# The fourth bank of x: normed one stage earlier, turned in 32 by 32 blocks by VectorE and re-laid by DMA instead of by TensorE transposes

## The chip, the cores and the metric

One NeuronCore of one Trainium2 chip runs the whole program in a single launch. The metric is the device time of an execution in microseconds (us). The kernel before takes 2167.93 us as the median of three runs (2167.46 to 2168.04). The profile comes from one more execution, which took 2169.86 us, of which 2168.0 us lie between its first and its last instruction; that is the profile's span.

## The reference

A decoder block for one sequence of 2048 positions and a width of 1024, in float32:

```python
h = rms_norm(x, g_norm) * (1.0 + scale) + shift        # scale, shift from c @ w_mod
proj = h @ w_in                                        # (2048, 1024) @ (1024, 8192)
x_rnn, z_rnn, q, k, v, z_attn, g_r, g_a = split(proj)
# branch A: causal conv, gated linear recurrence over the positions, SiLU gate, w_out_rnn
# branch B: rotary q and k, three dilated windows of attention, SiLU gate, w_out_attn
merged = sigmoid(g_r + bg_r) * y_rnn + sigmoid(g_a + bg_a) * y_attn
x = rms_norm(x + gate * (merged @ w_o), g_final)
```

What matters here is `h`. TensorE contracts over the partitions, so the projections need `h` with its 1024 columns on the partitions and the positions along the free dimension, while `x` lies in memory with the positions as rows. Before the projections, each row of `x` is scaled by its reciprocal root mean square (the norm), the matrix is turned, and each column gets its factor `g` and its shift `s`.

## The kernel before

**Tiles.** The 2048 positions are four banks of 512. A bank is read as four tiles `xs[r]` of 128 positions by 1024 columns, r being the position modulo 4. Column block `k` (0 to 7, 128 columns) of a bank becomes one turned tile of 128 partitions (columns) by 512 positions, in the order r, j. Every operand of a product is kept as a high part (`float32r`, rounded) and a low part (what is left), and each product is three matmuls (line 152): high by high, high by low, low by high.

**Halves and stages.** The work on `w_in` is done twice: `f = 0` for banks 0 and 1, `f = 1` for banks 2 and 3. Each half has these stages:

- *Values* (`values_half`, line 876): the 1024 columns of `v` for both banks, as wide products with `h` as the stationary operand. Weights come by SP's queue into the five tiles R (line 473), and are split by ScalarE (line 160) and GpSimd (line 166) into the seven tiles S. In the same stage the second bank of the half is built (`build_odd`, line 588): its eight column blocks, and from them and the first bank the sums T1 to T4 that the seven products of a Strassen scheme need.
- *Recurrent, gates, plain q and k*: 22 pairs of column tiles, each as seven products of 12 matmuls (`strassen`, line 349).
- *Rotated* (from line 1353): six pairs, 42 products, two of them q and k columns that get the rotary angles. Its order is written out by hand: `late` maps the number of finished products to functions, `later(d, fn)` puts `fn` behind the d-th product from now, and after each product `run_late` (line 220) issues what is due; then come the loads and splits of the next weights (`pump`). So each engine's queue has its instructions in exactly this order, and an instruction that has to wait holds up what stands behind it on its engine. In the second half this stage computes the residual gate; in the first half it prepares bank 2, the first bank of the second half: `next_norm` loads it 3 products in, squares at 7 to 10 (line 1293), scales at 14 to 17 (line 1297), and `next_even` (line 1302) turns and builds it from product 36 on, so that the second half's values can start without a pause.

**The fourth bank before.** Bank 3 is loaded at line 1327 (`load_x`, line 541) when the second half begins. `norm_x` (line 545) norms it during the second half's values: four squares on ScalarE (line 549), the small steps of `rstd` on VectorE, four scalings on VectorE (line 551). Then `turned` (line 555) has TensorE transpose the four 128 by 128 pieces of one column block into PSUM (line 561), 32 transposes for the bank, and `build` (line 564) reads the PSUM tile twice on ScalarE, for the high part (line 571) and for a full copy that is kept (line 574), and has VectorE subtract (line 169). The order of the values stage is not written by hand: a planner orders its instructions by its own estimates of durations, per engine. The first half's odd bank, bank 1, takes the same path.

**After it.** Attention, the output projections and the final norm follow; their order is written by hand too, and counted in products and units, not in time.

The PSUM tiles of the Strassen products are X (two buffers), Z, W, V and Y (one each). V is written by product 4 of a pair, evicted, and then used once more by the pair's last product, which runs as the second product of the next pair; the next V follows two products behind that.

Of the kernel before, what the change touches and what calls it, by code (L numbers as in the profile page):

```python
# [90 lines left out]
def decoder_block(ctx, tc, x, c, positions, g_norm, w_mod, b_mod, w_in, b_gate, conv_w, conv_b,  # L91
# [10 lines left out]
    def scratch(name, shape):  # L102
        return nc.dram_tensor(name, shape, F32, kind="Internal").ap()
# [13 lines left out]
    gateD = scratch("gateD", [1, D])  # L117

    tabD = scratch("tabD", [2, 2, 32, HALF])

    sD = scratch("sD", [REBUILT * 7, P, 2, KH, P])

# [45 lines left out]
    def lo_dve(o, i, h):  # L168
        return nc.vector.tensor_tensor(o, i, h.bitcast(F32), ALU.subtract).ins  # L169
# [375 lines left out]
    def norm_x(st, xs, nb=2):  # L545
        for t in xs:
            jk = T(st, [P, D], BF16, "hf", bufs=nb)
            ss = T(st, [P, 3, 1], F32, "ss", bufs=4)
            nc.scalar.activation(jk[:], t, AF.Square, accum_out=ss[:, 0])
            rstd(ss)  # L550
            nc.vector.tensor_scalar(t, t, ss[:, 1], None, ALU.mult)
# [12 lines left out]
    def build(st, names, xs, k, first=False, keep=None, pt=None):  # L564
# [11 lines left out]
        else:  # L576
            hf = T(st, [P, CH], F32, "hf", bufs=2)
            nc.vector.tensor_scalar(hf[:], pv, g, s, ALU.mult, ALU.add)
            (lo_dve if k % 3 == 0 else lo_pool)(hl[:, k % KH, :], hf[:], hh[:, k % KH, :])

    def operand(name):
        B[name] = (slot(), slot())

# [1 line left out]
        for k in ks:  # L585
            build(st, ("B11", "B21"), xs, k, first)

    def build_odd(st, xs):

        B["B12"] = (T(st, [P, KH, CH], F32R, "b12h"), T(st, [P, KH, CH], F32R, "b12l"))  # L590
        operand("B22")
        f32 = lambda b, i, k: B[b][i][:, k, :].bitcast(F32)
        tt = nc.vector.tensor_tensor
        h = [T(st, [P, CH], F32, "hx", bufs=KT)[:] for _ in range(KT)]
        for k in range(KH):
            for k2 in (k, KH + k):
                build(st, ("B12", "B22"), xs, k2, keep=h[k2])
            yield
        for name in ("T1", "T2", "T3", "T4"):
            operand(name)  # L600

        def split(name, k, t):
            hh, hl = B[name]
            hi_act(hh[:, k, :], t)
            lo_dve(hl[:, k, :], t, hh[:, k, :])

        for k in range(KH):
            h1, h2 = h[k], h[KH + k]
            t = T(st, [P, CH], F32, "t0", bufs=2)[:]
            tt(t, h2, h1, ALU.subtract)  # L610
# [5 lines left out]
            tt(h2, h2, h1, ALU.subtract)  # L616
# [259 lines left out]
    def values_half(f, xs):  # L876

        n0, n1 = banks(f)
        if f:
            first = wide_values(vx, 0, n0, (0, 1))  # L880
            for _ in range(2):
                next(first)
            norm_x(vx, xs)
        else:
            for j in range(KH):
                store_values(vx, 0, n0, j, pv0[j])
            with tc.issue_after(last_copy[0]):
                norm_x(vx, xs)
            first = ()
        odd = build_odd(vx, xs)  # L890
# [12 lines left out]
        assert next(odd, None) is None  # L903
# [343 lines left out]
    def later(d, fn):  # L1247

        late.setdefault(n_prod[0] + d, []).append(fn)
# [32 lines left out]
            later(30 + 2 * q, lambda q=q: total(q))  # L1282
            later(31 + 2 * q, lambda q=q: bias(q))

    def next_norm():

        xs = []
        later(3, lambda: xs.extend(load_x(xp, 2, "x", 2)))
        ss = T(xp, [P, 3, 4], F32, "ss")

        def square(r):
            jk = T(xp, [P, D], BF16, "hf", bufs=2)
            nc.scalar.activation(jk[:], xs[r], AF.Square, accum_out=ss[:, 0, r : r + 1])

        for r in range(4):
            later(7 + r, lambda r=r: square(r))
            later(14 + r, lambda r=r: nc.scalar.activation(xs[r], xs[r], AF.Copy, scale=ss[:, 1, r : r + 1]))
        later(11, lambda: rstd_first(ss))
        later(12, lambda: rstd_last(ss))
        return xs  # L1300

    def next_even():

# [901 lines left out]
```

## Time and profile before

| | |
|---|---|
| runs | 2167.46, 2167.93, 2168.04 us |
| profiled execution | 2169.86 us, span 2168.0 us |
| TensorE (PE) busy | 2138.5 us, 99% of the span |
| VectorE (DVE), ScalarE (ACT), GpSimd (POOL) busy | 1495.3, 1295.4, 1111.4 us |
| rotated stage of the first half | about 571 to 689 us |
| values stage of the second half | about 689 to 781 us |

PE is TensorE's matmuls and PEld its weight loads. SP is the engine that issues most DMAs and does nothing else; SPq names its queue. A row of the timeline has the start, the duration, engine, line, operation, output and input, the number of instructions, and in brackets how long the engine had been idle and what ended that. A matmul's end is modelled, so neighbouring matmuls overlap in the rows: the step from one start to the next is what a matmul costs. A row of the table by stretches has the two ends and the length, then each engine's busy time and the number of its instructions, those that reach over the edges among them.

### The profile page before, as it was taken

What the parts mean: (1) busy time and instruction counts of PE and PEld (TensorE: products, weight loads), DVE (VectorE), ACT (ScalarE), POOL (GpSimd) and SP (SyncE); (2) the same over time, 40 slices, a digit from 0 to 9 for tenths busy, and PEclk for the clock granted to TensorE, in tenths of its full rate; (3) what the DMA queues carried; (4) which work ended last, traced back from release to release, by engine and by line L of the source; (5) the groups of instructions that cost most, each with busy time, mean ns of one, the idle gap of its engine ahead of it and who ended that gap; (6) DMA issues with size and microseconds to landing.
All of it is one profiled execution on the core that took longest, in us unless ns stands there. A gap on an engine that the chain in (4) does not pass through costs nothing.

```text
span 2168.0 us, 32583 instructions
## 1 busy us (share of the span) xinstructions
PE 2138.5 (99%) x10538; PEld 1788.4 (82%) x10539; DVE 1495.3 (69%) x2590; ACT 1295.4 (60%) x2591; POOL 1111.4 (51%) x868
## 2 busy tenths in 40 slices
PE   9999999999999999999999999999999999999998
PEld 6888788888888888888888887888888988878886
DVE  6759877768656725544446584677777787688887
ACT  5748668668644537557547522777877877444333
POOL 1467667677666322223224664466666564422444
PEclk9999999999999999999999999999999999999999
DMA  8467887886655378899996667889886777898553
GB/s 301 144 209 260 278 296 266 284 302 222 175 116 166 113 244 286 294 311 308 326 322 212 161 162 212 279 260 281 263 270 212 244 230 235 298 321 293 181 171 111
DMA packets 416431, 521.39 MB, mean 240 GB/s; under 512 B 107558, under 2 KB 282882, under 8 KB 415236
## 3 DMA queue, kind: packets, MB, share of 16 engines
q1 hardware_dynamic: 376244, 401.65, 59.6%
q10 hardware_dynamic: 34384, 99.78, 12.2%
q0 software_dynamic: 5632, 17.88, 2.5%
q8 instruction: 83, 1.36, 0.2%
q14 instruction: 88, 0.72, 0.1%
HBM read 332.02 MB, written 187.17 MB: 239 GB/s over the span
## 4 chain that ended last, share of the span: by engine, by line
PE 66%; DVE 6%; DMA 5%; ACT 2%; issue 2%; POOL 1%; SPq 0%; POOLq 0%; ACTq 0%; DVEq 0%
PE X L152 13%; PE V L152 13%; PE pj L152 9%; PE Z L152 7%; PE W L152 7%; PE Y L152 6%; PE sc L152 4%; PE o L152 4%; PE pg L152 1%; DMA fg<-mrT 1%; PE pT L1560 1%; DMA fg<-gaT 1%; PE pT L1573 1%; DVE ptl L169 1%; DVE yl L169 1%
## 5 line engine op out<-in xcount | busy, mean ns | idle before, releaser
L166 POOL TENSOR_TENSOR S<-R,S 128x512 fp32r<-128x512 f32 x192 | 295.3, 1545 | 170.1 <-ACT S L160 90.5
L152 PE MATMUL X<-T,S 128*128 128x512 f32 x1344 | 323.9, 390 | 1.5 <-ACT u L385 1.3
L152 PE MATMUL pj<-yh,S 128*128 128x512 f32 x896 | 324.8, 404 | 0.3 <-DVE S L169 0.3
L152 PE MATMUL V<-T,S 128*128 128x512 f32 x1344 | 324.3, 390 | 0.5 <-DVE ev L455 0.5
L152 PEld LDWEIGHTS X<-T,S 128*128 128x128 f32 x1344 | 251.8, 188 | 56.3 <-ACT u L385 2.8
L152 PEld LDWEIGHTS V<-T,S 128*128 128x128 f32 x1344 | 252.0, 188 | 54.4 <-ACT S L160 0.9
L166 POOL TENSOR_TENSOR S<-s,S 128x512 fp32r<-128x512 f32 x116 | 170.4, 1469 | 148.1 <-ACT S L160 112.1
L152 PEld LDWEIGHTS pj<-yh,S 128*128 128x128 f32 x896 | 168.7, 189 | 30.3 <-DVE S L169 1.3
L152 PE MATMUL pj<-yl,S 128*128 128x512 f32 x448 | 176.2, 393 | 0.5 <-POOL yl L166 0.3
L1475 ACT ACTIVATE pp<-pp,st 128x256 f32<-128x256 f32 (+3 forms) x256 | 133.6, 523 | 67.4 <-DVE st L1474 66.1
L160 ACT ACTIVATE S<-s 128x512 fp32r<-128x512 f32 x124 | 77.3, 624 | 143.7 <-DVE s L285 93.2
L152 PE MATMUL W<-T,S 128*128 128x512 f32 x672 | 161.7, 390 | 0.0
L152 PE MATMUL Y<-T,S 128*128 128x512 f32 x672 | 161.6, 390 | 0.0
L152 PE MATMUL Z<-T,S 128*128 128x512 f32 x672 | 161.4, 389 | 0.0
L160 ACT ACTIVATE S<-R 128x512 fp32r<-128x512 f32 x200 | 121.4, 622 | 59.0 <-issue 15.2
L169 DVE TENSOR_TENSOR ptl<-pT,pth 128x384 fp32r<-128x384 f32 (+1 forms) x160 | 97.9, 629 | 76.1 <-ACT pth L160 73.8
L152 PEld LDWEIGHTS W<-T,S 128*128 128x128 f32 x672 | 126.0, 188 | 26.9 <-issue 0.9
L152 PEld LDWEIGHTS Z<-T,S 128*128 128x128 f32 x672 | 126.2, 188 | 26.1
L152 PEld LDWEIGHTS Y<-T,S 128*128 128x128 f32 x672 | 126.1, 188 | 26.1
L974 DVE SCALAR_TENSOR_TENSOR xc<-xr,par,xc 128x512 f32<-128x512 f32 x96 | 103.7, 1080 | 57.2 <-ACT xc L968 54.9
L166 POOL TENSOR_TENSOR s<-R,s 128x512 fp32r<-128x512 f32 x32 | 43.1, 1346 | 189.0 <-ACT s L160 176.4
L1540 ACT ACTIVATE pp<-pp,M 128x256 f32<-128x256 f32 (+3 forms) x256 | 118.0, 523 | 9.9 <-DVE M L1663 9.9
(416 smaller groups left out, 4929.1 us busy)
## 6 DMA issues: line engine op xcount, KB each, us to landing
sD<-S ACTq DMA_DIRECT2D x140, 512.0 KB, 3.7
S<-sD SPq DMA_DIRECT2D x140, 512.0 KB, 5.5
S<-wD SPq DMA_DIRECT2D x82, 512.0 KB, 5.6
R<-in_w_in_dram SPq DMA_DIRECT2D x144, 256.0 KB, 3.4
wD<-s ACTq DMA_DIRECT2D x64, 256.0 KB, 5.6
kraw<-kqT SPq DMA_DIRECT2D x32, 384.0 KB, 5.2
T<-in_w_mod_dram SPq DMA_DIRECT2D x16, 512.0 KB, 9.1
vN<-ev SPq DMA_DIRECT2D x32, 256.0 KB, 2.8
```

The lines of the kernel that those rows point to most:

```text
L152: nc.tensor.matmul(o, lhsT=l, rhs=r, start=st, stop=sp, **kw)
L160: nc.scalar.activation(o, i, AF.Copy)
L166: nc.gpsimd.tensor_tensor(o, i, h.bitcast(F32), ALU.subtract)
L169: return nc.vector.tensor_tensor(o, i, h.bitcast(F32), ALU.subtract).ins
L974: nc.vector.scalar_tensor_tensor(xc, xr[:, i : i + CH], cw(i), xc, ALU.mult, ALU.add)
L1475: nc.scalar.activation(pdst, pdst, AF.Exp, bias=m_, scale=-1.0, accum_out=l_)
L1540: nc.scalar.activation(pp, pp, AF.Copy, scale=w)
L1560: nc.tensor.transpose(pt[:, c0 + j * P : c0 + (j + 1) * P], pp[i][:, k * P : (k + 1) * P], ident)
L1573: nc.tensor.transpose(pt[:, c * P : (c + 1) * P], pp[:, half * P : (half + 1) * P], ident)
```

## The change

Bank 3 gets a scratch `xD` in HBM and takes another way.

1. In the first half's rotated stage, `next_norm` becomes `next_banks`. Bank 3 is loaded 1 product in, squared at 6 and 7 (two tiles each), `rstd` at 8 and 9, scaled by ScalarE at 10 and 11. At products 12 to 19, `turn_rows` takes one column block each: four VectorE transposes, which turn every 32 by 32 block in its place, into a tile `w` of two buffers (tag `hf`), and one DMA of `w` to `xD[k]` on SP's queue. Bank 2 then uses the same two tiles for x: it is loaded 20 products in, squared at 25 and 26, scaled at 30 and 31. `next_even` stays where it is.
2. At the start of the second half, `load_turned` reads `xD` in eight DMAs of 256 KB, each of which fills 32 partitions of one of two tiles in 512 byte pieces; that puts the blocks where the full transpose would have them, in another order along the free dimension. It takes the place of `load_x`.
3. `norm_x` and `turned` are gone from the second half's values. `build_turned` reads the loaded tile in SBUF: ScalarE makes the high part, VectorE makes the full copy (`tensor_scalar`, which ScalarE made before), and VectorE subtracts. The reordering of the free dimension is done by the access patterns of the two.

The first half's odd bank keeps the old path.

```diff
+    by_class = lambda ap: ap.rearrange("p (r b a) -> p r b a", r=4, b=4)
+    by_window = lambda ap: ap.rearrange("p (b r a) -> p r b a", r=4, b=4)
+
+    def turn_rows(st, xs, k):
+        w = T(st, [P, CH], F32, "hf", bufs=2)
+        for r in range(4):
+            nc.vector.transpose(w[:].rearrange("p (t r a) -> p r t a", t=4, r=4)[:, r], xs[r][:, k * P : (k + 1) * P])
+        nc.sync.dma_start(xD[k], w[:])
+
+    def load_turned():
+        xs = [T(hp, [P, KH, CH], F32, "T", bufs=14) for _ in range(2)]
+        for kh in range(2):
+            src = xD[kh * KH : (kh + 1) * KH].rearrange("k (b i) (t q) -> t i k b q", b=4, t=4)
+            for t in range(4):
+                nc.sync.dma_start(xs[kh][t * 32 : (t + 1) * 32].rearrange("p k (b q) -> p k b q", b=4), src[t])
+        return [x[:, k, :] for x in xs for k in range(KH)]
+
+    def build_turned(names, x, k, hf):
+        hh, hl = (t[:, k % KH, :] for t in B[names[k // KH]])
+        g, s = gs[:, k : k + 1], sh[:, k : k + 1]
+        nc.scalar.activation(by_class(hh), by_window(x), AF.Identity, bias=s, scale=g)
+        nc.vector.tensor_scalar(by_class(hf), by_window(x), g, s, ALU.mult, ALU.add)
+        lo_dve(hl, hf, hh)
...
-    def build_odd(st, xs):
+    def build_odd(st, xs, f):
...
-                build(st, ("B12", "B22"), xs, k2, keep=h[k2])
+                if f:
+                    build_turned(("B12", "B22"), xs[k2], k2, h[k2])
+                else:
+                    build(st, ("B12", "B22"), xs, k2, keep=h[k2])
...
                 next(first)
-            norm_x(vx, xs)
...
-        later(3, lambda: xs.extend(load_x(xp, 2, "x", 2)))
-            later(7 + r, lambda r=r: square(r))
-            later(14 + r, lambda r=r: nc.scalar.activation(xs[r], xs[r], AF.Copy, scale=ss[:, 1, r : r + 1]))
-        later(11, lambda: rstd_first(ss))
-        later(12, lambda: rstd_last(ss))
+        def norm(n, steps):
+            xs, ss = [], T(xp, [P, 3, 4], F32, "ss", bufs=2)
+            d, d_squares, d_scales = steps
...
+            later(d, lambda: xs.extend(load_x(xp, n, "x", 2)))
+            for r in range(4):
+                later(d_squares + r // 2, lambda r=r: square(r))
+                later(d_scales + r // 2, lambda r=r: scale(r))
+            later(d_squares + 2, lambda: rstd_first(ss))
+            later(d_squares + 3, lambda: rstd_last(ss))
+            return xs
+
+        x3 = norm(3, (1, 6, 10))
+        for k in range(KT):
+            later(12 + k, lambda k=k: turn_rows(xp, x3, k))
+        return norm(2, (20, 25, 30))
...
-            x1 = load_x(hp, 3, "T", 14)
+            x1 = load_turned()
...
-            x0 = next_norm()
+            x0 = next_banks()
```

More of the change, by code (lines that the diff above doesn't have):

```diff
@@ L119, in decoder_block @@
     tabD = scratch("tabD", [2, 2, 32, HALF])
+    xD = scratch("xD", [KT, P, CH])
     sD = scratch("sD", [REBUILT * 7, P, 2, KH, P])
@@ L889, in values_half @@
             first = ()
-        odd = build_odd(vx, xs)
+        odd = build_odd(vx, xs, f)
         for _ in first:
@@ L1283, in residual_gate, with next_banks, square, scale @@
             later(31 + 2 * q, lambda q=q: bias(q))
[L1285 to L1300 removed]
+    def next_banks():
+        def norm(n, steps):
+            xs, ss = [], T(xp, [P, 3, 4], F32, "ss", bufs=2)
+            d, d_squares, d_scales = steps
+            def square(r):
+                jk = T(xp, [P, D], BF16, "hf", bufs=2)
+                nc.scalar.activation(jk[:], xs[r], AF.Square, accum_out=ss[:, 0, r : r + 1])
+            def scale(r):
+                nc.scalar.activation(xs[r], xs[r], AF.Copy, scale=ss[:, 1, r : r + 1])
+            later(d, lambda: xs.extend(load_x(xp, n, "x", 2)))
[9 more added lines that the diff above has]
+        return norm(2, (20, 25, 30))
     def next_even():
```

## The prediction, made before the changed kernel ran

> **What bounds the kernel now.** I read the page's first part, then the table of engines by stretches, the waits of TensorE, the chain of waits, and the timeline around the fourth bank.
>
> ```profile
> PE 2138.5 (99%) x10538; PEld 1788.4 (82%) x10539; DVE 1495.3 (69%) x2590; ACT 1295.4 (60%) x2591; POOL 1111.4 (51%) x868
> ```
>
> ```profile
> core 0: us, PE busy (x) PEld busy (x) DVE busy (x) ACT busy (x) POOL busy (x), PEclk, DMA share, GB/s
> 571.16:681.39 110.23, 110.23 (x495) 91.31 (x494) 67.42 (x94) 46.47 (x79) 72.97 (x53) 1.00 0.59 146
> 705.58:727.07 21.49, 21.49 (x112) 17.70 (x111) 16.71 (x21) 16.37 (x27) 11.01 (x8) 1.00 0.42 124
> 727.07:748.16 21.09, 20.70 (x91) 16.82 (x90) 20.59 (x28) 10.79 (x19) 4.60 (x3) 1.00 0.33 100
> ```
>
> ```profile
> PE Z L152 <- ACT ev L857: 0.4, 1, 0.4
> ```
>
> TensorE is busy for 110.23 of 110.23 us in the rotated stage and for 21.49 of 21.49 us while bank 3 is transposed, at full clock. From 681 to 781 us it has one wait, 0.4 us for ScalarE's eviction (line 857). So the instructions of TensorE set the time here, and a removed one should shorten it by its own step, if nothing that feeds TensorE becomes late. Does that wait belong to the bank that is changed? The chain of waits answers:
>
> ```profile
> 709.10 0.78 ACT b12h L571
> 712.62 1.72 DVE t L610
> ...
> 737.97 0.70 DVE hx L616
> 738.69 0.04 ACT T L160
> 739.23 0.59 ACT ev L857
> 739.86 1.66 PE Z L152 x6
> ```
>
> It does. From ScalarE's read of the first transposes of bank 3 (709.10) the chain runs almost without a gap along VectorE's sums of `build_odd` from 712.62 to 738.67, then through ScalarE's copy behind them (line 160) to the eviction queued after that, and back to TensorE. VectorE is busy for 20.59 of 21.09 us there.
>
> **What leaves TensorE.** The 32 transposes.
>
> ```profile
> 697.42:705.58 8.16, 8.16 (x38) 1.00 0.40 127
> ```
>
> ```profile
> 705.58:727.07 21.49, 5.28 (x32) 4.13 (x32) 1.00 0.42 124
> ```
>
> ```profile
> 712.01 0.60 PE L561 MATMUL pg<-cs,T 128*128 128x128 f32 x4
> 712.36 1.63 PE L152 MATMUL X<-S,T 128*128 128x512 f32 x6
> ```
>
> The first fence is the table for TensorE's matmuls on the tiles T (length, busy time, matmuls, clock, DMA share, GB/s), the second the one for line 561 alone, the third the timeline. The clean stretch is six groups of six matmuls, and the other two of its 38 reach over its edge: 36 take 8.16 us, 0.2267 us each. The stretch with the transposes, in the table above, has 112, less the same two 110, less 32 transposes 78; 78 x 0.2267 = 17.68 us, and 21.49 - 17.68 = **3.81 us** are the transposes, 0.119 each. Four in a row, from 712.01 to 712.36, cost 0.35, which gives 8 x 0.35 = 2.80 as the lower bound; their modelled busy time, 5.28, overlaps and is only an upper bound. I take 3.81, which includes the switching between the kinds.
>
> The next stretch, 727.07 to 748.16, holds 15 groups of six matmuls: 90 x 0.2267 = 20.40 of 21.09 us, so **0.69 us** hang on the wait. The chain begins 11 us earlier in the changed kernel, since the norm goes:
>
> ```profile
> L551 DVE TENSOR_SCALAR T<-T,ss 128x1024 f32<-128x1024 f32 x4 | 4.0, 1018 | 0.0
> L578 DVE TENSOR_SCALAR hf<-pg,gs,mod 128x512 f32<-128x512 f32 x8 | 6.5, 810 | 7.9 <-ACT T L571 7.9
> L574 ACT ACTIVATE hx<-pg,mod,gs 128x512 f32<-128x512 f32 x5 | 4.0, 793 | 0.0
> ```
>
> ```profile
> 684.07 1.05 SPq L541 DMA_DIRECT2D T<-in_x_dram  x2
> 696.00 1.04 ACT L549 ACTIVATE hf<-T 128x1024 bf16<-128x1024 f32 x1
> 705.91 0.76 DVE L551 TENSOR_SCALAR T<-T,ss 128x1024 f32<-128x1024 f32 x1
> ```
>
> Squares to last scaling take 696.00 to 706.67 us. ScalarE loses four squares (4 x 1.04 = 4.2) and eight copies (8 x 0.79 = 6.3); VectorE loses four scalings (4.0) and the small `rstd` steps, and gains eight `tensor_scalar` of 512 columns, from 0.51 each (half of line 551) to 0.81 (line 578, reading PSUM): 4.1 to 6.5, I take 5. So VectorE's work is about the same and starts some 11 us earlier, and I count the 0.69 as gained. If the planner puts another such wait in its place, it is 0 (below, a rival).
>
> **What the load costs.** Eight DMAs of 256 KB instead of two of 1 MB, on SP's queue, ahead of the weights of the values.
>
> ```profile
> 573.60 1.90 SPq L1102 DMA_DIRECT2D Ct<-tabD  x4
> Ct<-tabD SPq DMA_DIRECT2D x4, 128.0 KB, 5.3
> ```
>
> ```profile
> 725.19 3.48 POOL L166 TENSOR_TENSOR S<-R,S 128x512 fp32r<-128x512 f32 x2 [3.06 <-PE X L152]
> 754.44 2.54 POOL L166 TENSOR_TENSOR S<-R,S 128x512 fp32r<-128x512 f32 x2 [3.34 <-ACT S L160]
> ```
>
> A DMA into 32 partitions takes SP 0.48 us to issue (1.90 for four) and lands in 5.3 us. So SP is held 8 x 0.48 = 3.8 instead of 1.05 us, and weights behind it are up to 2.8 us later; the tile is there near 684 + 3.8 + 5.3 = 693, ahead of the 706.67 of now. What hides the 2.8 us: GpSimd's split at 725.19 had waited 3.06 us for TensorE to free a tile, so the weights run ahead of TensorE, not behind. I take 0.
>
> [...]
>
> **What the rotated stage takes on.** Scaling and squares of bank 3, 32 VectorE transposes, eight stores.
>
> ```profile
> L1082 DVE STREAM_TRANSPOSE ev<-ev x1: 702/702/702, 282.6 to 282.6; 128x512 f32<-128x512 f32 x1
> L1057 DVE TENSOR_SCALAR an<-an 128x128 f32<-128x128 f32 x2 | 0.4, 218 | 0.0
> L1297 ACT ACTIVATE x<-x,ss x4: 1137/1138/1142, 605.9 to 614.5; 128x1024 f32<-128x1024 f32 x4
> ```
>
> ```profile
> 584.76:601.08 16.32, 16.32 (x74) 13.52 (x72) 11.07 (x17) 10.38 (x18) 13.30 (x10) 1.00 0.59 161
> 601.08:622.84 21.76, 21.76 (x98) 18.02 (x96) 14.00 (x22) 12.14 (x19) 13.56 (x10) 1.00 0.64 129
> ```
>
> A 512 column transpose takes 0.70 us, so four of 128 columns take between 0.70 (by columns) and 4 x 0.70 = 2.8 (if it were all overhead). The nearest row of 128 by 128 is 0.218, hence 0.87 per product and 7.0 in all. Products 12 to 19 are the stretch 601.08 to 622.84, where VectorE has 21.76 - 14.00 = 7.76 us to spare: it just fits. ScalarE has 10.38 of 16.32 us in products 6 to 11, four squares in it; the four scalings add 4 x 1.14 = 4.6, so 14.9 of 16.3: it fits too. Bank 2's own steps move to products 20 to 31, and are first read at product 36, five products (13.6 us) behind its scaling.
>
> The queue is the tight place. SP's stores stand in program order, each waits for its product's VectorE transposes, and behind it wait the q stores and the raw weights.
>
> ```profile
> 608.55 0.69 DVE L1145 TENSOR_TENSOR t<-t,t 128x512 f32<-128x512 f32 x1
> 612.16 0.69 DVE L455 TENSOR_TENSOR t<-V,u 128x512 f32<-128x512 f32 x1 [1.21 <-PE V L152]
> ```
>
> ```profile
> 612.99 2.51 SPq L1150 DMA_DIRECT2D kqT<-t  x4
> 712.40 0.93 SPq L858 DMA_DIRECT2D vN<-ev  x2
> vN<-ev SPq DMA_DIRECT2D x32, 256.0 KB, 2.8
> ```
>
> ```profile
> 617.56 2.72 PE V L152 x12
> ```
>
> SP is already late there: the store at 612.99 was ready at 609.24, 3.75 us before. Eight more, at 0.47 (the vN row) to 0.63 (the kqT row), add 3.8 to 5.0 us over 21.8. The tile `w` has two buffers, so a transpose waits until the store two products back has landed: SP's 3.75 + 2.8 to land + 0.87, less two products (5.44), puts VectorE 2.0 us late, not growing from one to the next while SP keeps up. What stands behind on VectorE are evictions of PSUM. The nearest deadline is V: evicted by 612.85, needed again at 617.56, 4.7 us to spare. So 2.0 us are hidden, and I take 0; the bounds are 0 and, with the longer lateness below, several us.
>
> [...]
>
> **The sum.** 3.81 + 0.69 + 0 + 0 = 4.50 us off the profiled execution's 2169.86 us: 2165.36. It stands 1.93 us above the median of the runs; the same gain there gives 2167.93 - 4.50 = **2163.43 us**. What follows (Strassen pairs, attention, output) is ordered by products and keeps its distance.
>
> **Rivals.**
>
> *The wait stays or comes back elsewhere.* For it: ScalarE's queue is planned anew, and an eviction can again be put behind a copy that waits for VectorE. Against it: VectorE is 11 us earlier. Gain 3.81: 2164.12.
>
> *The weights become late in the values.* The place is SP's queue at 684 us: 2.8 us from the eight loads, and GpSimd's 0.94 (3.48 - 2.54) on a pair of splits. For it: both are new in one stretch. Against it: GpSimd waits for TensorE. 3.7 us lost, 0.8 gained: 2167.1.
>
> *The transposes were free.* TensorE may have filled with them time in which the weights were not yet there; then removing them leaves a wait of the same length: 2167.9. Against it: no wait of TensorE on S in the clean stretch before, at 0.2267 a matmul.
>
> *Slower: SP and VectorE hold each other up in products 12 to 19.* Were the stores to land like the slowest of the weights here,
>
> ```profile
> DMA to landing us min/median/max: 2.0/2.8/7.7
> ```
>
> in 7.7 us, and SP 3.75 + 5.0 = 8.75 late, VectorE would come 8.75 + 7.7 + 0.87 - 5.44 = 11.9 us late; less the 4.7 to spare TensorE stops for 7.2 us at V, and at the V seven products on again: 14.4 - 4.5 = 9.9 us slower, 2177.8. It decides against the change from a total stall of 4.5 us on.
>
> **How the numbers follow.** The forecast has 0.52, the wait that stays 0.20, late weights 0.12, free transposes 0.06, the slower case 0.10. The forecast's own range is 2162.6 to 2164.1. The range reaches down to 2162.0 for small waits that go as well, and up to 2168.0, which takes in the next three cases. Beyond 0.2% (4.34 us, about what a measurement of this kernel can tell from no change) faster means below 2163.59, and the forecast lies just past it: I give 0.8 of its chance to faster, 0.42. The slower case ends beyond the bound for 0.08; its rest and the other cases make 0.50 within.
>
> **What would show it.** Right: line 561 has 96 transposes, not 128; TensorE without a wait from 571 to 681 us; the values stage 4.5 us shorter, with no eviction behind a copy that waits for VectorE; VectorE's 128 by 128 transposes near 0.22 us. Wrong: a wait of TensorE on V or on S near products 14 to 25, or on S behind the eight loads; transposes far above 0.22 us; the total shift unlike that of the values stage.

## The result, and the profile after

The changed kernel takes 2177.64 us (median; 2174.53 to 2181.04) against 2168.70 us beside it on the same chip: a ratio of 1.0035, 95% interval 1.0025 to 1.0045. It is **slower**, and above the forecast range. Its profiled execution took 2175.55 us (before: 2169.86), with a span of 2173.8 us (2168.0). The medians are 8.94 us apart and the two profiled executions 5.69; what follows accounts for the second of these.

The first part of its page, and the waits of TensorE from 600 to 800 us (in total, times, longest):

```profile
PE 2139.5 (98%) x10507; PEld 1787.8 (82%) x10507; DVE 1502.7 (69%) x2608; ACT 1294.7 (60%) x2584; POOL 1119.8 (52%) x868
```

```profile
PE X L154 <- POOL S L168: 3.1, 2, 2.4
PE V L154 <- DVE t L457: 1.8, 1, 1.8
PE Z L154 <- ACT ev L889: 0.8, 1, 0.8
```

The transposes are gone from TensorE (31 fewer matmul records), yet it is busy 1.0 us longer. In place of one wait of 0.4 us it has 5.7 us of waits, on V in the rotated stage and on the split weights S and an eviction in the values stage. The table by stages (length, then busy time of TensorE, weight loads, VectorE, ScalarE, GpSimd, then clock) shows why it is busy longer:

```profile
571.16:681.39 110.23, 108.40 (x476) 89.03 (x475) 74.99 (x128) 52.92 (x89) 68.54 (x49) 0.98 0.67 170
705.00:727.00 22.00, 18.12 (x66) 13.75 (x65) 19.70 (x25) 13.37 (x23) 16.49 (x6) 0.85 0.41 118
```

The granted clock is 0.98 and 0.85 where it was 1.00 in both stretches.

To see where the time went I read the start of the same matmuls in both traces. The timeline has the last rotated product of the first half (V) and the first product of the second half's Strassen pairs (X), in the kernel before,

```profile
685.91 3.00 PE L152 MATMUL V<-T,S 128*128 128x512 f32 x12
...
781.39 2.88 PE L152 MATMUL X<-T,S 128*128 128x512 f32 x12
```

and in the changed one:

```profile
690.76 2.99 PE L154 MATMUL V<-T,S 128*128 128x512 f32 x12
...
788.64 2.88 PE L154 MATMUL X<-T,S 128*128 128x512 f32 x12
```

I call the time between the two the values stage: 95.48 us before, 97.88 after, so **2.40 us longer where 4.50 shorter was forecast**. The first rotated product starts 0.89 us later, the last one 4.85: the rotated stage lost 3.96 us, where 0 was forecast. Behind the values stage 1.45 us come back. 0.89 + 3.96 + 2.40 - 1.45 = 5.80 us, the difference of the spans. The 0.89 is nothing of the change: a wait of TensorE on VectorE's eviction near 300 us, in unchanged code, is 1.52 us long here and absent in the profile before. In the kernels below it is anything from absent to 2.98 us, and 0.35 and 2.98 in two executions of one and the same kernel (e5 and e11). Where the 1.45 comes from stays open.

**The rotated stage.** VectorE's and SP's rows of the timeline, with TensorE's at the stall:

```profile
612.16 0.89 DVE L590 STREAM_TRANSPOSE hf<-x 128x128 f32<-128x128 f32 x4 [0.19 <-DMA xD<-hf]
615.55 0.89 DVE L590 STREAM_TRANSPOSE hf<-x 128x128 f32<-128x128 f32 x4 [1.83 <-DMA xD<-hf]
618.59 2.53 SPq L1213 DMA_DIRECT2D kqT<-t  x4
621.00 0.89 DVE L590 STREAM_TRANSPOSE hf<-x 128x128 f32<-128x128 f32 x4 [2.79 <-DMA xD<-hf]
621.22 1.05 SPq L591 DMA_DIRECT2D xD<-hf  x2
625.54 0.89 DVE L590 STREAM_TRANSPOSE hf<-x 128x128 f32<-128x128 f32 x4 [3.07 <-DMA xD<-hf]
631.35 4.61 PE L154 MATMUL V<-T,S 128*128 128x512 f32 x12 [1.83 <-DVE t L457]
```

Four transposes take 0.89 us, as forecast. But five of the eight groups wait for a store to land before they get their buffer, and from the third to the sixth the wait grows: 0.19, 1.83, 2.79, 3.07 us (the eighth waits 0.88). The stores wait in SP's queue behind the q stores, which themselves wait for VectorE. At the end an eviction of V comes some 9 us late (620.32 us before, 630.62 now; 1.08 of the difference is the shift that TensorE has already) and TensorE stops for 1.83 us. TensorE's table from its restart on (length, busy, clock) shows a second part of the price:

```profile
631.35:633.00 1.65, 1.65 (x4) 0.58 0.98 303
633.00:634.50 1.50, 1.50 (x5) 0.50 0.64 132
634.50:636.00 1.50, 1.50 (x7) 0.82 0.92 288
636.00:638.00 2.00, 2.00 (x10) 1.00 1.00 246
```

The clock is at one half for 3.4 us in all: twice what the rows' means lack of 1.00, times their lengths (1.65 x 0.42 + 1.50 x 0.50 + 1.50 x 0.18 = 1.71). Finer rows of the same table have 0.50 from 631.7 to 634.9 and 1.00 ahead of 631.5 and from 635.1 on. It is back 3.7 us after the restart. The product behind starts 3.72 us later than its shift up to there: 1.83 of wait and 1.9 of clock.

**The values stage.** The load of the turned tile (SP), ScalarE's first read of it, GpSimd's weight splits and TensorE's wait:

```profile
693.17 1.70 SPq L599 DMA_DIRECT2D T<-xD  x3
694.96 1.23 SPq L1213 DMA_DIRECT2D kqT<-t  x2
696.24 2.32 SPq L599 DMA_DIRECT2D T<-xD  x3
698.65 1.29 SPq L1213 DMA_DIRECT2D kqT<-t  x2
699.99 1.18 SPq L599 DMA_DIRECT2D T<-xD  x2
...
706.92 2.94 ACT L606 ACTIVATE T<-T,mod,gs 128x512 fp32r<-128x512 f32 x4 [8.93 <-DMA T<-xD]
710.51 16.50 POOL L168 TENSOR_TENSOR S<-R,S 128x512 fp32r<-128x512 f32 x6 [7.50 <-ACT S L162]
718.62 0.96 PE L154 MATMUL X<-S,T 128*128 128x512 f32 x3 [2.37 <-POOL S L168]
```

The eight loads stand between q stores on SP and go out over 8 us instead of 3.8; the tile is read at 706.92, not 693. (Counted from the last rotated V that is 16.2 us, where 7.1 was forecast and the first read of transposes before, at 709.10, came after 23.2.) ScalarE waits 8.93 us for it, with copies of weights queued behind, GpSimd 7.50 us for these. And then one split takes 8 us. The same line's instructions from 700.5 to 727 us (ns min/median/max), before and after:

```profile
L166 POOL TENSOR_TENSOR S<-R,S x10: 1276/1738/1839, 700.5 to 726.9; 128x512 fp32r<-128x512 f32 x10
```

```profile
L168 POOL TENSOR_TENSOR S<-R,S x8: 1295/1720/8057, 700.2 to 725.3; 128x512 fp32r<-128x512 f32 x8
```

Behind these waits TensorE runs at half clock again, in one stretch:

```profile
720.37:727.20 6.83, 6.05 (x14) 0.50 0.71 202
```

A matmul's step is 0.453 us there (six of them from 722.27 to 724.99) and was 0.227 at 1.00 (six from 700.90 to 702.26), so 6.05 us of work at half clock are 3.0 us lost. With the 3.9 us of waits that is 6.9 of the 7.5 us by which the stage is longer than in the kernels below that have no wait in it (2.40 + 5.09).

### The profile page after: what moved, and what is told of

Same layout as the page of the kernel before. It is cut to its first block, busy times and chain, and to the rows that moved or that the text cites. A ratio compares the mean times of both kernels' runs of the same rounds, so it can differ in the third digit from the quotient of the medians.

```text
span 2173.8 us, 32545 instructions
## 1 busy us (share of the span) xinstructions
PE 2139.5 (98%) x10507; PEld 1787.8 (82%) x10507; DVE 1502.7 (69%) x2608; ACT 1294.7 (60%) x2584; POOL 1119.8 (52%) x868
## 4 chain that ended last, share of the span: by engine, by line
PE 59%; DVE 5%; DMA 3%; ACT 2%; issue 1%; POOL 1%; SPq 0%; POOLq 0%; ACTq 0%; DVEq 0%
PE pj L154 11%; PE X L154 11%; PE V L154 10%; PE Z L154 6%; PE W L154 6%; PE Y L154 5%; PE sc L154 4%; PE o L154 4%; PE pT L1600 1%; PE pg L154 1%; PE pT L1613 1%; DVE ptl L171 1%; ACT pp L1515 1%; DVE pp L1514 1%; DVE yh L165 1%
## 5 line engine op out<-in xcount | busy, mean ns | idle before, releaser
L168 POOL TENSOR_TENSOR S<-R,S 128x512 fp32r<-128x512 f32 x192 | 302.0, 1581 | 164.0 <-ACT S L162 100.5
```

What stands on the lines that cost most here:

```text
L168: nc.gpsimd.tensor_tensor(o, i, h.bitcast(F32), ALU.subtract)
```

## The experiments

All are timed against the kernel before on the same chip. "Rotated" and "values" are TensorE's waits in 571 to 690 and 690 to 800 us, "split" is GpSimd's longest S<-R in 690 to 745 us, "stage" the length of the values stage against 95.48 us, as above. The last four columns are of the one profiled execution, which need not be the median one: that of e2 took 2179.37 us, that of e3 2173.79.

| kernel | median us | ratio, 95% interval | rotated | values | split | stage |
|---|---|---|---|---|---|---|
| before | 2168.70 | 1 | 0 | 0.4 | 1.84 | 0 |
| changed | 2177.64 | 1.0035 [1.0025, 1.0045] | 1.8 | 3.9 | 8.06 | +2.40 |
| e1_actq | 2174.01 | 1.0016 [1.0007, 1.0026] | 0.4 | 2.3 | 8.08 | +0.95 |
| e2_rot | 2175.43 | 1.0021 [1.0012, 1.0031] | 4.5 | 1.2 | 1.79 | +1.12 |
| e3_order | 2178.14 | 1.0036 [1.0023, 1.0049] | 2.5 | 3.5 | 1.81 | -0.74 |
| e4_both | 2175.43 | 1.0026 [1.0016, 1.0036] | 0 | 5.6 | 10.19 | +3.35 |
| e5_dvelo | 2167.23 | 0.9987 [0.9978, 0.9996] | 0 | 0 | none | -5.09 |
| e6_load2 | 2170.70 | 1.0003 [0.9993, 1.0012] | 0 | 1.3 | 8.16 | -2.56 |
| e7_actcopy | 2174.02 | 1.0019 [1.0010, 1.0029] | 0 | 3.6 | 3.45 | +1.71 |
| e8_dvelo_load2 | 2166.58 | 0.9989 [0.9980, 0.9998] | 1.1 | 0 | none | -5.08 |
| e9_before_dvelo | 2169.08 | 0.9994 [0.9984, 1.0003] | 0 | 0 | none | -0.71 |
| e10_after_dvelo | 2169.56 | 1.0001 [0.9992, 1.0009] | 1.2 | 0 | none | -4.72 |
| e11_dvelo5 | 2167.30 | 0.9989 [0.9980, 0.9998] | 0 | 0 | none | -5.09 |
| e12_hold | 2177.52 | 1.0035 [1.0022, 1.0049] | 5.4 | 0.4 | 1.84 | +0.01 |
| e13_space1 | 2173.57 | 1.0015 [1.0006, 1.0025] | 0 | 3.2 | 1.82 | +0.77 |
| e14_space128 | 2174.71 | 1.0022 [1.0013, 1.0031] | 0 | 5.0 | 1.74 | +2.05 |
| e15_chain | 2175.06 | 1.0023 [1.0013, 1.0034] | 0 | 3.3 | 1.81 | +0.83 |
| e16_hidve | 2166.93 | 0.9986 [0.9976, 0.9995] | 0 | 0 | 1.75 | -5.10 |
| e17_chain_dvelo | 2167.58 | 0.9988 [0.9978, 0.9997] | 0.9 | 0 | none | -5.08 |

### The store's queue, the rotated part alone, the order (e1 to e4)

e1_actq moves the store of the turned tile to ScalarE's queue, one product later:

```
-        nc.sync.dma_start(xD[k], w[:])
+        later(1, lambda: nc.scalar.dma_start(xD[k], w[:]))
```

> One edit against the changed kernel: the eight stores of turned tiles are issued from ScalarE's queue, one product behind their transposes, and no longer from SP's queue. The theory: the rotated stage loses 3.7 us (the V product of the changed kernel falls from 1.08 to 4.80 us behind) because VectorE waits for a buffer of w, whose store stands late in SP's queue, and SP in turn waits for VectorE. Then VectorE's waits for the stores (8.8 us in all) nearly go, TensorE's wait of 1.83 us at V goes, and the kernel is about 3.7 us faster than the changed one: some 3 to 5 us above the kernel before. Rival: the 32 transposes, 0.27 us each instead of 0.22, are too much for VectorE by themselves (8.6 us against 7.8 us to spare): then TensorE still waits at V and the time stays 7 to 8 us above the kernel before.

The stall is gone (0.4 us of wait for 1.8), with the same 32 transposes: one wait for a buffer is left, 1.2 us in the trace, where 8.8 us in five were. So the stall of the rotated stage is the pair of two buffers and SP's queue, not the transposes. In the twelve runs with this edit TensorE's waits in the stage are 0 to 1.1 us; in the four with the stores on SP (changed, e2, e3, e10) they are 1.2 to 4.5. The values stage still loses, and its one split of 8.08 us is the same.

e2_rot keeps the rotated part and leaves the second half in its old way:

```
-            x1 = load_turned()
+            x1 = load_x(hp, 3, "T", 14)
...
+            norm_x(vx, xs)
-        odd = build_odd(vx, xs, f)
+        odd = build_odd(vx, xs, 0)
```

> The rotated stage as in the changed kernel, with the norm, the transposes and the stores of bank 3, whose result is then not used; the second half loads, norms and transposes bank 3 on TensorE as the kernel before does. The theory of two stalls: the wait at V stays, with its slow matmuls behind it, and the values stage is that of the kernel before: 3.5 to 5 us above the kernel before. Rival, all the loss is in the values stage and the wait at V was an accident of one execution: within 1 us of the kernel before.

The rotated part alone costs 0.21% and stalls for 4.5 us (1.8 at the same V, 1.2 at a later one, 1.5 at the building of bank 2). e3_order takes the changed kernel and puts the builds of bank 3 two steps later, behind the weights' copies on ScalarE; e4_both is e1 and e3:

```
         for _ in first:
-            next(odd)
+            pass
         for ws in wide_values(vx, 1, n0, (0, 1), None if f else ws1):
-            next(odd)
+            with tc.issue_after(last_hi[0]) if f else ExitStack():
+                next(odd)
```

> One edit against the changed kernel: bank 3's builds start two steps later, behind ScalarE's splits of the next weights, so that ScalarE's queue no longer stands at a build that waits for the load of the turned tiles while weights wait behind it. The theory: the values stage loses 7 us (4.5 us of gain became 2.45 us of loss) by this order; then TensorE's waits on S (3.1 us) go and the time is 0 to 2 us above the kernel before, the wait at V remaining. Rival: the weights are late because the turned load, in pieces of 512 bytes, slows their own DMAs (5.4 us to land in the place of 2.9) and VectorE slows GpSimd; then the waits on S stay and the time is at least 5 us above.

> Both edits together, stores from ScalarE's queue and the later builds. If the two stalls are all that was lost, the 32 transposes of TensorE come out as forecast: 3.5 to 4.5 us below the kernel before. If something else of the change costs time (the load, VectorE's added work, another wait), 0 us or above.

The order alone gains nothing. In e3 TensorE's wait moves from the splits to ScalarE's evictions. e4 is the plainest picture of what happens to GpSimd: ScalarE's copies of weights now come on time, and one split still takes 10.19 us. The instructions of that line from 706 to 722 us, and GpSimd's and VectorE's rows (the first two and the last two of VectorE's row there):

```profile
L170 POOL TENSOR_TENSOR S<-R,S x4: 1257/1483/10191, 707.0 to 720.0; 128x512 fp32r<-128x512 f32 x4
```

```profile
706.92 0.68 DVE L173 TENSOR_TENSOR T<-hx,T 128x512 fp32r<-128x512 f32 x1
706.97 14.30 POOL L170 TENSOR_TENSOR S<-R,S 128x512 fp32r<-128x512 f32 x4 [2.37 <-PE V L154]
707.52 0.68 DVE L646 TENSOR_TENSOR hx<-hx,T 128x512 f32<-128x512 f32 x1
...
715.35 0.68 DVE L647 TENSOR_TENSOR hx<-hx,T 128x512 f32<-128x512 f32 x1
716.07 1.64 DVE L650 TENSOR_TENSOR hx<-hx,hx 128x512 f32<-128x512 f32 x1
```

VectorE's two-input operations start every 0.60 us from 706.92 to 715.35. GpSimd's split begins at 706.97 and ends at 717.17. The first step that is longer (0.72, to 716.07) stands where it gets through, and VectorE's operation there takes 1.64 us instead. The last split takes 1.26 us, with VectorE idle. In the other three splits of 8 us (changed, e1, e6) the first slow operation of VectorE stands behind a step of 0.71 to 0.73 too. But GpSimd does not always need such a step: in the kernel before, a split that begins at 725.19 gets in behind a step of 0.61, since the operation of VectorE there is the slow one.

```profile
725.13 0.69 DVE L613 TENSOR_TENSOR hx<-hx,T 128x512 f32<-128x512 f32 x1
725.74 1.79 DVE L169 TENSOR_TENSOR b12l<-hx,b12h 128x512 fp32r<-128x512 f32 x1
```

So the traces show that a row of such operations can keep a split out; what decides when it gets in stays open.

In e4 the long split reaches TensorE by another way than ScalarE's copies. SP stands at a load of raw weights until the split has freed their tile, a store of the values (vN) stands behind that load, and ScalarE's eviction waits for the store:

```profile
703.19 14.32 SPq L477 DMA_DIRECT2D R<-in_w_in_dram  x3
717.61 0.39 SPq L892 DMA_DIRECT2D vN<-ev  x1
721.23 0.60 ACT L891 ACTIVATE ev<-X 128x512 f32<-128x512 f32 x1 [7.54 <-DMA vN<-ev]
721.88 5.49 PE L154 MATMUL X<-S,T 128*128 128x512 f32 x12 [5.63 <-ACT ev L891]
```

In the changed kernel and in e1 the chain of waits also runs through the split of 8 us, then a load of raw weights (2.5 and 2.6 us), ScalarE's copy of them and the eviction of Z behind it.

### The tile's load, the copy, and the split (e5 to e9)

e6_load2 is e1 with the tile loaded in two transfers as it lies (bank 3's positions then stand in another order). e7_actcopy is e1 with the full copy on ScalarE. e5_dvelo is e1 with the low parts of the second half's value weights by VectorE; e9_before_dvelo is the same edit on the kernel before; e8 is e5 with e6's load.

```
-            for t in range(4):
-                nc.sync.dma_start(xs[kh][t * 32 : (t + 1) * 32].rearrange("p k (b q) -> p k b q", b=4), src[t])
+            nc.sync.dma_start(xs[kh][:], xD[kh * KH : (kh + 1) * KH].rearrange("k p c -> p k c"))
```

```
-        nc.vector.tensor_scalar(by_class(hf), by_window(x), g, s, ALU.mult, ALU.add)
+        nc.scalar.activation(by_class(hf), by_window(x), AF.Identity, bias=s, scale=g)
```

```
-            ws = w if x == 0 and w else load_wide(q, kh)
+            ws = w if x == 0 and w else load_wide(q, kh, lo_dve if n > 1 else lo_pool)
```

> The kernel with the stores on ScalarE's queue, and one edit: in the second half's values the low parts of the weights are made by VectorE and no longer by GpSimd. The theory now: the values stage loses because VectorE's sums of bank 3, which start earlier and run without gaps, hold up GpSimd's splits of the weights (2.97 us each from 705 to 717 us with VectorE busy for 11.93 of 12 us; 1.53 in the kernel before), so that TensorE waits for weights and then runs at half clock. Without GpSimd in that stage TensorE's waits on S go, VectorE's subtractions fall from 1.7 to 0.7 us, and the time falls by 3 us or more against the kernel with the stores alone, to within 1 us of the kernel before or below it. Rival, the turned load delays the weights (5.6 us to land): the waits on S stay and nothing is gained. Other rival, VectorE is overfilled: TensorE waits for the odd bank or for evictions, and it is slower.

> The kernel with the stores on ScalarE's queue, and the turned tiles loaded in two DMAs of 1 MB, 2 KB pieces over all partitions, instead of eight in 512 byte pieces: the re-laying is left out, so the positions of bank 3 stand in another order, and all later work is the same. If the turned load holds up the weights (SP's queue, and their landing in 5.6 us instead of 2.9), TensorE's waits in the values stage go and it is 3 us or more faster than with the stores alone. If VectorE's hold on GpSimd decides, the waits stay and the time is within 1 us.

> The kernel with the stores on ScalarE's queue, and the full copy of bank 3 made by ScalarE again, not by VectorE's tensor_scalar. If it is the eight tensor_scalar from SBUF (0.47 us each, 3.8 in all) that hold GpSimd up, its splits get shorter than 2 us on the mean and about 1 to 2 us come back. If it is VectorE's subtractions of two SBUF tiles, GpSimd's splits stay near 2.1 us and the time is the same or, with ScalarE's queue fuller by 6 us ahead of the weights, slower by up to 3 us.

> Control: the kernel before with the low parts of the second half's value weights on VectorE. There GpSimd kept up, TensorE's only wait in the stage is 0.4 us, so the theory expects no gain: within 1 us of the kernel before, or slower, if VectorE (20.6 of 21.1 us busy) is overfilled. If it is faster by 2 us or more, the edit is a gain of its own and says nothing on the change.

e7 changes nothing in the time, though its longest split is 3.45 us and not 8.08. It also gives ScalarE eight more operations, so it does not show what the eight new `tensor_scalar` cost; but in the changed kernel, in e1 and in e4 none of them runs beside the long split. e6 gains about 3 us on e1 (2174.01 to 2170.70; the runs of before beside them differ by 0.26): ScalarE waits 2.63 us for the tile and not 6.72. e5 gains 6.8 us on e1 and is faster than the kernel before, while the control e9 is not: what the split on GpSimd costs, it costs only together with the change.

> e5_dvelo with the load of the normed tile in two transfers of 1 MB as they lie (the re-lay left out: bank 3's positions then stand in another order, which changes the output and not the work). Theory of the held-up split: with VectorE making the low parts no TensorE wait is left in the values stage, so the load's form is worth nothing more: 2167.2, within 1. Theory of the late weights: the eight transfers still cost something that the waits do not show, and the time is 1 to 3 lower.

With no split on GpSimd the load's form is worth nothing more (e8 as e5). So the late tile and the slow split are no two sums to add: on e1 (+0.95) the load's form gives back 3.5 us of the stage, the split 6.0, and both together no more than the split alone.

### Do the two stalls add, and what does a wait cost? (e10 to e12)

e10 is the changed kernel, its stores on SP, with e5's edit; e11 is e5 again. e12_hold is the kernel before with additions of VectorE ahead of an eviction of V:

```
+            nc.vector.memset(w[0][:], 1.0)
+            for _ in range(17):
+                nc.vector.tensor_tensor(w[1][:], w[0][:], w[0][:], ALU.add)
```

> The changed kernel as it is (stores on SP) with one edit: VectorE makes the low parts of the second half's value weights. Theory: the two stalls are separate and their costs add. Then the rotated stage stalls as in the changed kernel (the wait of TensorE on VectorE's t of about 1.8 us near 631, 3.7 us by the start of the next product), the values stage has no wait left, and the time is that of e5_dvelo plus 3.7: 2170.9 (2169.5 to 2172.3). Rival: the two belong to one late chain, and without the split on GpSimd the whole is as e5_dvelo: 2167.2. Second rival: the values stage was late because the rotated stage left it late; then it stays at about 2175.

> The same kernel as e5_dvelo, again, in five rounds: 2167.2 if the gain over the kernel before (1.9 us) holds; 2169 if it was chance.

> The kernel before with 17 additions of 128x512 and one memset put on VectorE in the rotated stage, just ahead of the eviction of product 18's V, about 10.6 us of VectorE work and nothing else. V of product 22 needs that buffer: a wait of TensorE of about 2 us near 629 is forced. If a wait lowers the granted clock after it, the clock is near 0.5 for some us after the wait, the start of product 23 moves by about twice the wait (3.5 to 5 us), and the time is about 2173. If a wait costs only itself, the start of product 23 moves by the wait alone (about 2 us) at clock 1.00, and the time is 2171.

They are separate. e10 has no wait in the values stage and still one in the rotated stage, 1.25 us on a later V, for a split of ScalarE's: its median is 2.3 us above e11's. That is less than the 3.7 expected, since this execution has no stall at the V near 631 and its clock stays at 1.00 behind the other; the products behind come about 1.5 us later. In e12 17 additions took 13.37 us and not 10.6, and TensorE waits 5.42 us and not 2:

```profile
635.89 4.62 PE L152 MATMUL V<-T,S 128*128 128x512 f32 x12 [5.42 <-DVE t L455]
```

```profile
631.50:633.00 1.50, 0.00 (x0) 0.85 0.00 0
633.00:634.50 1.50, 0.00 (x0) 0.50 0.00 0
634.50:636.00 1.50, 0.11 (x1) 0.50 0.00 0
636.00:638.00 2.00, 2.00 (x5) 0.50 0.78 177
638.00:642.00 4.00, 4.00 (x16) 0.83 0.84 201
```

The product behind starts 7.32 us later: 5.42 and 1.9 of clock. So the clock's part is about the same after 1.83 and after 5.42 us of waiting, neither nothing nor a doubling, the two that had been thought of. But 1.9 is no fixed price. Twice what these rows lack of 1.00 makes 6.8 us at half clock, two times the 3.4 of the changed kernel; about half of them pass while TensorE still waits. In thirteen such stretches, out of ten of the traces, the half clock lasts 3.4 us (six of them) or 6.8 (seven), whatever the length of the wait, and begins 0.8 to 4.2 us after TensorE has stopped. Among them are 3.4 us from 1637.1 in the trace of before, 3.4 from 631.6 and from 1638.6 and 6.8 from 720.4 in the changed kernel. By the two steps above, 0.453 and 0.227 us, half of the part that falls on work is lost.

Nor does every wait bring it. In e2 TensorE waits at the same V as in the changed kernel, for 1.80 us and not 1.83, and the clock stays:

```profile
632.61 3.02 PE L154 MATMUL V<-T,S 128*128 128x512 f32 x12 [1.80 <-DVE t L457]
```

```profile
632.61:640.00 7.39, 7.39 (x32) 1.00 0.92 264
```

In all the traces each of the ten waits from 2.24 us on brought the half clock (among them 2.24 in e16, 2.37 in the changed kernel, 2.89 in e7, 4.45 in e14, 5.42 in e12 and 5.63 in e4); of those between 1.4 and 2.2 us some did (1.83 in the changed kernel, 2.14 in e13, 2.15 in e15) and some did not (1.80 in e2, 2.07 in e3, 2.13 in e4). So in this range the length of a wait alone did not decide it, and the 1.9 us that the changed kernel's stall cost on top are those of its profiled execution.

### Shut-out or order? (e13 to e17)

Is the 8 us split the cause, or one sign of it? e15_chain is e1 with VectorE's sums held in the order of the text; e13 and e14 add a memset of one and of 128 columns behind each of them (e15 has only the first half of the edit):

```
+            with tc.issue_after(last[0]) if last[0] else ExitStack():
+                i = fn(*args)
...
+            with tc.issue_after(i):
+                last[0] = nc.vector.memset(spacer[:], 0.0).ins
```

> Control for the two that follow: e1_actq with the two-input operations of VectorE in the second half's odd builds held in the order of the text, nothing else. Both theories: one of GpSimd's weight splits still takes about 8 us (8.08 in e1_actq), TensorE waits 2 to 4 us in the values stage, and the time is that of e1_actq, 2174 (2171.5 to 2176).

> e15_chain with a one-column memset of VectorE behind each of those operations; the work for GpSimd, the load and the order stay. Theory of the shut-out: GpSimd's split gets no turn while two-input operations of VectorE follow each other without a break, and any break lets it in: no split is over 2.2 us, TensorE's waits on S go, and the time is 2168 to 2170. Rival, late weights alone: the split's length was a sign of late data and not the cause; with the load as late as before TensorE's waits and the time stay at 2174. Second rival: a break has to be longer than one column takes, then this run is as e15_chain and the next one is not.

> As e13_space1 with memsets of 128 columns, some 0.1 to 0.2 us each over 48 places, 5 to 10 us more of VectorE work in the stage. Shut-out: no split over 2.2 us; the time 2168 to 2172, the more work of VectorE taking back some of it. Late weights alone: 2174 or more.

The control itself took the long split away (1.81 us for 8.08; in its order VectorE waits some 0.7 us for ScalarE behind several sums, which may be what lets GpSimd in); so the memsets could show nothing of the shut-out, and e13's 1.82 us is not their work. But the time stayed, and that refuted what I held by then, that the shut-out alone makes the loss. In e15 TensorE waits 3.3 us, all of it for evictions, that of Z above all:

```profile
PE Z L154 <- ACT ev L899: 2.2, 1, 2.2
```

```profile
708.32 1.77 DVE L171 TENSOR_TENSOR T<-hx,T 128x512 fp32r<-128x512 f32 x1
710.02 1.78 DVE L171 TENSOR_TENSOR b12l<-hx,b12h 128x512 fp32r<-128x512 f32 x1
...
714.24 0.63 ACT L162 ACTIVATE T<-t 128x512 fp32r<-128x512 f32 x1 [5.73 <-DVE t L628]
714.78 1.13 ACT L162 ACTIVATE S<-R 128x512 fp32r<-128x512 f32 x2
715.82 0.58 ACT L899 ACTIVATE ev<-Z 128x512 f32<-128x512 f32 x1
```

In e15 no split takes over 1.81 us, and VectorE's operations beside them take 1.77 us instead of 0.68. Its sums come late, ScalarE waits 5.73 us for one, and the eviction of Z stands behind. Two more runs part the two accounts. e16_hidve is e15 with the sums' high parts rounded on VectorE, so that ScalarE waits for no sum; e17_chain_dvelo is e15 with e5's edit.

```
-            hi_act(hh[:, k, :], t)
+            spaced(nc.vector.tensor_copy, hh[:, k, :], t) if f else hi_act(hh[:, k, :], t)
```

> e15_chain with the high parts of the second half's odd sums rounded by VectorE instead of ScalarE, so that nothing on ScalarE waits for VectorE any more; the load, GpSimd's splits and the order of VectorE's sums stay, and VectorE has 16 operations more. Theory: in e15_chain TensorE waits 3.3 us because the evictions stand behind ScalarE's copies of sums, and these sums run late behind a tile that lands near 701. Then the waits on ScalarE's evictions go (3.3 to under 0.5 us) and the time falls by 4 to 5 us, to 2169.5 to 2171. Rival: with the tile late, any order only moves the stall (to GpSimd's splits shut out by VectorE's longer row, or to TensorE's operands behind the added VectorE work), and the time stays at 2174 to 2176.

> e15_chain with the low parts of the second half's value weights by VectorE, as in e5_dvelo: the same edit with another order. Theory that VectorE's and GpSimd's operations slow each other (1.77 instead of 0.68 us on VectorE in e15_chain, 1.5 to 8 us on GpSimd): VectorE's operations are all 0.68 us, the waits are 0 to 0.5 us, and the time is that of e5_dvelo, 2167.3 (2166 to 2169). Rival, e5_dvelo gained by the order of ScalarE's queue alone: 2172 to 2175.

**Both** take all waits of the values stage away, and it is 5.10 and 5.08 us shorter; e16 lands below its forecast of 2169.5 to 2171. e16 leaves the splits on GpSimd, with VectorE's operations at 1.77 us beside them and a tile first read at 703.14 (700.67 in e15); e17 leaves the copies where they were. So neither account is the cause alone. In e15's order the loss needs both VectorE and GpSimd slowing each other and ScalarE's queue that passes the lateness on to evictions; take one away and the stage has slack. Where a split is shut out for 8 us or more, ScalarE's order alone is no cure: e4 loses by SP's queue. The third link, the late tile, was never removed whole; e6, which took part of it, got back half of the stage.

e16 is the fastest, 2166.93 us, 0.14% under the kernel before (0.05 to 0.24%), with e5 and e17 not to be told from it. But its stage gained 5.10 us and the whole 2.9. Some of it is lost at the change to attention, where e16 has a wait of 2.24 us and the profile of before another one, of 1.25 (on ScalarE's `kq`):

```profile
1351.19 0.50 PE L154 MATMUL pj<-yh,S 128*128 128x512 f32 x1 [2.24 <-DVE fg L1824]
```

The chain of waits runs there through two loads in a row (4.69 and 7.14 us). This wait is 1.3 to 2.2 us in e5, e11, e16 and e17, 1.4 in the changed kernel and 0.8 in e9, which is earlier too. Why it is there, and the rest of the difference, stays open.

## Why the prediction was wrong

- **What leaves TensorE** was right and a little low. Without waits the stage is 5.09 us shorter in e5 and e11 and 5.10 in e16. The control e9, where only the old 0.4 us wait is gone, has 0.71 of it (0.69 forecast), so the transposes were 5.09 - 0.71 = 4.38 us (3.81 forecast). They were not free: that rival falls.
- **"The tile is there near 693"** failed, and with it the 0 for the load and the 11 us head start of the chain. The issue time of a DMA was nearly right (0.54 us, 0.48 forecast), but SP's queue also holds the rotated stage's q stores, which wait for their data: 8 us for the loads, and a first read 16.2 us behind the last rotated V, 9 us later than forecast. Of the 11 us head start 7 were left (16.2 against 23.2). They did not help, since what came late was not the chain of sums but the weights.
- **"GpSimd's split had waited 3.06 us for TensorE, so the weights run ahead"** was true of before and no cover. The new wait is on ScalarE, ahead of the weights' copies, a queue that the step on the load left out. The rival of late weights had the right stage and GpSimd in it, at 3.7 us; the stage lost 2.40 + 5.09 = 7.5 us against what it could do. Its price for GpSimd, 0.94 on a pair, came from a pair of 3.48 us, 1.74 for each split, where the changed kernel has one of 8.06.
- **VectorE beside GpSimd** was looked for in the wrong operations. In the values stage the eight `tensor_scalar` were counted as VectorE's new work (5 us); none of these runs beside the long split in the changed kernel, e1 and e4. The two-input sums, which the kernel before has too, are what runs there, and the split takes 8.06, 8.08 and 10.19 us.
- **"2.0 us late, not growing"** failed. The waits of VectorE went 0.19, 1.83, 2.79, 3.07, since SP's q stores wait for VectorE and VectorE for SP: each round trip adds. The 4.7 us to spare at V did not cover 9 us, and the rotated stage lost 3.96 us where I took 0. I had the loop as the slower rival, at the right place (V) and with a chance of 0.10; its price came out of the slowest landing, where landing was 2.8 us and the growth did it. That its time, 2177.8, lies at the measured 2177.64 is luck: it has two stalls of 7.2 us at V and a values stage 4.5 us shorter, and the run has one of 1.83 at V and a values stage 2.40 longer.
- **The price of a wait.** Every stall was priced at its length. In the changed kernel the clock added 1.9 us in the rotated stage and 3.0 in the values stage.
- **The rivals were kept apart.** Two happened at once, late weights and the loop of SP and VectorE, and a wait on ScalarE's eviction came back as well (0.8 us in the changed kernel, 1.4 in e1, 3.3 in e15). A range that ended at 2168.0 had no room for two.

## What to carry to other kernels

A step that feeds the bound engine from a longer way round (store, reload, other engines) is to be priced by when its data lands, with every item of each in-order queue on the way, waits of these items included; slack read off the old trace is slack in the old order. Before moving work to a stage, look whether VectorE's two-input operations will then follow each other without a pause: such a row kept one split of GpSimd's going for its whole length here (8 to 10 us, though not in every order). A stall of TensorE above 2.2 us cost half clock as well each time here, and one of 1.4 to 2.2 us in some executions only; its price here was its length and half of the time at half clock (3.4 or 6.8 us) that fell on work, 1.9 and 3.0 us in the changed kernel.

## What the runs showed of the hardware

- GpSimd's 128x512 subtraction (1.26 us in e4 with VectorE idle) took 8.06 (changed kernel), 8.08 (e1), 8.16 (e6) and 10.19 us (e4) beside back-to-back two-input operations of VectorE, over eleven (changed kernel) to fourteen (e4) of these in a row. Elsewhere beside such operations it took about 1.7 us (median 1.74 from 700 to 727 us in the kernel before), and VectorE's 0.68 us is then 1.63 to 1.79.
- Half clock (0.50 where the rows beside it have 1.00) came in stretches of 3.4 or 6.8 us, beginning 0.8 to 4.2 us after TensorE stopped, after each wait from 2.24 us on and some of those between 1.4 and 2.2. A wait of 1.83 us in the changed kernel brought it, one of 1.80 in e2 did not; what decides it in this range is not shown.
- A VectorE transpose of 128x128 in 32 by 32 blocks takes 0.27 us (263 to 312 ns over 32 in the changed kernel), and four in a row 0.88 to 0.89 us.
